# Merge gates of an encoder layer: the sigmoid moved from the merge to the gate projection, as exp, plus one and reciprocal

## The chip, the cores and the metric

The kernel runs on one core of a Trainium2 chip. The core has a matrix engine (TensorE, called PE in the profile; its weight loads have a row of their own, PEld), VectorE (DVE), ScalarE (ACT), GpSimd (POOL) and SyncE (SP), whose queue here issues most DMA transfers. Each engine works through its own instructions in a fixed order and waits on semaphores for the others. PE writes its results to PSUM, from where ACT or DVE must copy or add them out before the same bank is used again.

The metric is the device time of one execution in microseconds. A profile is one such execution, recorded instruction by instruction.

## What is computed

One inference step of one encoder layer for 1024 prompt positions and 64 sample positions (1088 in all), model width 1024. One combined projection of the normalised input gives queries, keys and values, two recurrent inputs, memory queries and, in its last 3072 columns, the logits of three merge gates. Three branches (stick-breaking attention, a gated linear recurrence, cross-attention into a memory) are each projected back to the model width and merged by sigmoid gates, one gate per branch, position and channel:

```python
proj = xn @ lw["w_in"]
...
g = jax.nn.sigmoid(gates.astype(jnp.float32) + lw["b_merge"].astype(jnp.float32)).reshape(b, t, N_BRANCH, D_MODEL)
merged = (g[:, :, 0] * (o_sb @ lw["w_br_sb"]) + g[:, :, 1] * (o_lru @ lw["w_br_lru"])
          + g[:, :, 2] * (o_mem @ lw["w_br_mem"])).astype(x.dtype)
x = x + merged @ lw["w_out"]
```

A SwiGLU feed-forward block follows. All data are float32.

## The kernel before

**Layout and product.** Channels lie on the 128 partitions and positions along the free dimension; a row of 128 channels has T = 1088 positions, in two halves of HT = 544, each of two pieces of HC = 272. Every large product is made with a Strassen-like scheme of seven products instead of eight, on pairs of output rows (256 channels): `sw_weights` (line 149) loads the weights of a pair through SyncE, forms their sums on DVE and splits each into a high and a low part (ACT copies, DVE subtracts: `split`, lines 70 to 73). `sw_steps` (line 182) runs the seven products as fourteen steps, two pieces each, and yields after every step, so that a caller can put other work in between. Line 192 is the matmul. The first three products leave PSUM by an ACT copy into a temporary tile (`keep`, line 202); the other four go through `done`, which calls the caller's `out` for the piece and, after the second piece, the caller's `after` for the half row. All of that stands under `tc.high_priority()`.

Two PSUM pairs are used in turn, so a product needs the pair that was emptied one product earlier. Temporaries are tiles named `swt`; four places serve them in turn and a pair takes two, so two pairs are in flight.

**The projection stage.** `pair_stream` (line 799) runs 24 pairs: eight for the recurrent inputs, four for the memory queries, and last twelve for the merge gates (three branches of four pairs). Its `out` adds the evicted piece to the temporary on DVE (line 809) or copies it out on ACT (line 811). Its `after` stores the half row to a scratch tensor in DRAM on SyncE's queue (line 817): `xl_scr`, `gl_scr`, `q_scr`, and for the gates `g_scr[b][row]`, as raw logits. The weights of the next pair are asked for before the steps of the present one.

The steps of this stream are woven into other work by `bulk.run(n)`: into the eight blocks of the recurrence (lines 860 to 925; each uses ACT's Sigmoid, Tanh, Exp, Sqrt and Gelu) and into the four heads of the memory attention (`mem_attn`, line 982), three steps per token tile. There, `scores` takes a row maximum on DVE (L997), scales it (L999), lets ACT compute the Exp (L1002) and normalises on DVE with a reciprocal (L1003) and a multiply (L1004); `queries` does the query norm (L975 on PE, L977, L244 and L979 on DVE, L245 on POOL). The gate pairs begin in the last block of the recurrence and run through all four heads and beyond. PE's and all other engines' order is fixed when the program is built, by a list scheduler that takes priorities and estimated durations; the hardware doesn't reorder.

**The merge stage.** For each branch and pair of rows, `branch_pair` (line 1124) loads the four half rows of gate logits back (L1128, tiles `sig`, four buffers of the pool tag `stg`) and applies the Sigmoid on ACT with the bias per channel, a column of `prm` from PB = 0 on (L1130). It then runs the projection of the branch; its `out` multiplies each piece by its gate, on POOL after a DVE add (L1136, L1137) or on DVE (L1139), and adds it to `mg` on POOL (L1141). A gate buffer is free for the next pair once its two pieces have been multiplied. After the third branch `form_operands` (line 1096) makes the operands of the output projection from `mg`.

**Table loads.** ACT keeps one set of activation functions at a time; the build puts an ACT_TABLE_LOAD ahead of a function of another set. The profile lists them under the line of the function that needs them.

Of the kernel before, what the change touches and what calls it, by code (L numbers as in the profile page):

```python
# [10 lines left out]
F32 = mybir.dt.float32  # L11
F32R = mybir.dt.float32r
BF16 = mybir.dt.bfloat16
AF = mybir.ActivationFunctionType
ALU = mybir.AluOpType
# [3 lines left out]
P = 128  # L19
D = 1024  # L20
KT = D // P
# [7 lines left out]
MH = 4  # L29
# [7 lines left out]
CQ, CK, CV, CXL, CGL, CQM, CGATE = 0, 1024, 2048, 3072, 4096, 5120, 6144  # L37
# [6 lines left out]
HT = T // 2  # L44
# [5 lines left out]
def kernel(ctx: ExitStack, tc: tile.TileContext, x_prompt, x_sample, mem_prompt, cache_sb_k, cache_sb_v,  # L50
# [6 lines left out]
    V, S, G, TE = nc.vector, nc.scalar, nc.gpsimd, nc.tensor  # L57
    LD, ST = nc.scalar, nc.sync

    cst = ctx.enter_context(tc.tile_pool(name="cst", bufs=1))  # L60
# [121 lines left out]
    def sw_steps(W, X, n, banks, temp, out, mid=None, after=None, fswap=0, hswap=0):  # L182


        def run(op, bank, start):
            a, b = PAIRS[op]
            for c in range(2):
                cs = slice(c * HC, (c + 1) * HC)
                for i in range(n):
                    w, x = W[a], X[b][i]  # L190
                    for j, (wj, xj) in enumerate(((0, 0), (0, 1), (1, 0))):
                        TE.matmul(bank[c][:, :HC], w[:, wj, i], x[:, xj, cs], start=start and i == 0 and j == 0,  # L192
                                  stop=i == n - 1 and j == 2, skip_group_check=True)
                yield c

        def part(j, c=None):
            s = j % 2 * HT + (c or 0) * HC
            return tmp[j // 2][:, s:s + (HT if c is None else HC)]

        def keep(bank, c, j):  # L200
            with tc.high_priority():
                S.copy(part(j, c), bank[c][:, :HC])  # L202

        def done(f, half, bank, c, j):
            with tc.high_priority():
                out(f ^ fswap, half ^ hswap, c, bank[c][:, :HC], part(j, c), j < 3)
                if c and after:
                    after(f, half, part(j))

        bx, bw = banks(), banks()  # L210
        tmp = [temp(), temp()]
        for c in run(0, bx, True):
            keep(bx, c, 0)
            yield
        for c in run(1, bw, True):
            keep(bw, c, 1)
            yield
        for c in run(2, bx, False):
            keep(bx, c, 2)
            yield  # L220
        for c in run(3, bw, False):
            if c == 0 and mid:
                mid()
            done(1, 0, bw, c, 2)
            yield
        for c in run(4, bx, False):
            done(1, 1, bx, c, 1)
            yield
        by = banks()
        for c in run(5, by, True):  # L230
            done(0, 0, by, c, 0)
            yield
        for c in run(6, bx, False):
            done(0, 1, bx, c, 3)
            yield

    def sw_product(*a, **k):
        for _ in sw_steps(*a, **k):
            pass
# [35 lines left out]
    xl_scr = [drm.tile([P, T], F32, name=f"xl{k}") for k in range(KT)]  # L275
    gl_scr = [drm.tile([P, T], F32, name=f"gl{k}") for k in range(KT)]
    q_scr = [drm.tile([P, T], F32, name=f"q{k}") for k in range(KT)]
# [22 lines left out]
    prm = cst.tile([P, 152], F32, name="prm")  # L300
    PB, PCW, PCB, PBA, PBX, PAL, PSC, PSH, PQG = 0, 24, 56, 64, 72, 80, 88, 112, 120
    PNM, PNF, PNE = 128, 136, 144
    tail = cst.tile([P, 8, KT], F32, name="tail")
    clog = cst.tile([P, 8], F32, name="clog")
    nclog = cst.tile([P, 8], F32, name="nclog")


    with ExitStack() as c1:
# [15 lines left out]
        for t in range(NTOK):  # L324
            n = P if t < 8 else DSEQ
# [11 lines left out]
        for g in range(3):  # L337
            for t in range(3 * g, 3 * g + 3):
                xt, n = xts[t]
# [5 lines left out]
            w = min(384, T - c0)  # L345
            for k in range(KT):
                tg = ("z", "tr")[k % 2]
                p = ps.tile([P, 512], F32, tag=tg, name="xp", bufs=3 if tg == "z" else 2)
                for j in range(3):
                    xt, n = xts[3 * g + j]  # L350
                    TE.transpose(p[:, j * P:j * P + n], xt[:n, k * P:(k + 1) * P], ident[:n, :n])
                gk = prm[:, PNM + k:PNM + k + 1]
                for a, b in ((c0, min(c0 + w, HT)), (max(c0, HT), c0 + w)):
                    if a < b:
# [4 lines left out]
                                               op0=ALU.mult, op1=ALU.subtract)  # L359
# [308 lines left out]
        pt = ps.tile([P, 512], F32, tag="tr", name="prt1", bufs=2)  # L668
        TE.transpose(pt[:, :122], pr1[:122, :], ident[:122, :122])
        V.tensor_copy(prm[:, :122], pt[:, :122])  # L670

        def x_sums():

            for i in range(KT // 2):
                def quarter(k, half):
                    q = sb.tile([P, HT], F32, tag="xq", name=f"xq{k}{half}", bufs=3)
                    u = xq(k, half)
                    V.tensor_add(q, f32(u[:, 0]), f32(u[:, 1]))
                    return q

                k0, k1 = 2 * i, 2 * i + 1
                t3 = quarter(k1, 1)
                yield
                t1 = quarter(k0, 1)
                yield
                V.tensor_sub(t3, t3, t1)
                ST.dma_start(s_scr[i]["T3"], t3)
                yield
                t2 = quarter(k0, 0)
                yield  # L690
                V.tensor_sub(t1, t1, t2)
                ST.dma_start(s_scr[i]["T1"], t1)
                yield
                V.tensor_add(t2, t2, t3)
                ST.dma_start(s_scr[i]["T2"], t2)
                yield
                t4 = quarter(k1, 0)
                yield
                V.tensor_sub(t4, t4, t2)
                ST.dma_start(s_scr[i]["T4"], t4)  # L700
                yield
# [27 lines left out]
    NI = KT // 2  # L729
# [26 lines left out]
    def half(name):  # L756
        return wpl.tile([P, HT], F32, tag="stg", name=name, bufs=4)
# [3 lines left out]
    def operand_at(oi, i, name):  # L761
        return at(UNITS[oi * NI + i], name).rearrange("p (x n) -> p x n", x=2)
# [15 lines left out]
    X = {o: A.get(o, []) for _, o in PAIRS}  # L778
    for oi, (_, o) in enumerate(PAIRS):
        if o[0] == "T":  # L780
            for i in range(NI):
                t = operand_at(oi, i, f"x{o}{i}")
# [6 lines left out]
    def temp():  # L789
        return at(cycle("t", TEMPS), "swt", F32)  # L790
# [8 lines left out]
    def pair_stream(pairs, last):  # L799

        def weights(i):
            if i == len(pairs):
                return last()
            cols, _, nm = pairs[i]
            return sw_weights([w_in[0, :, c:c + P] for c in cols], nm, w_slot, w_stage)

        def out(f, hf, c, p, t, add):
            if add:
                V.tensor_add(t, p, t)  # L809
            else:  # L810
                S.copy(t, p)

        w = weights(0)
        for i, (_, dst, _) in enumerate(pairs):
            wn = weights(i + 1)
            yield from sw_steps(w, X, NI, banks4, temp, out,
                                after=lambda f, hf, t: ST.dma_start(dst[f][:, hf * HT:(hf + 1) * HT], t))
            w = wn
        stream["w"] = w

    stream = {}
    pairs = [((CXL + n * P, CGL + n * P), (xl_scr[n], gl_scr[n]), f"wl{n}_") for n in range(KT)]
    pairs += [((CQM + 2 * m * P, CQM + (2 * m + 1) * P), (q_scr[2 * m], q_scr[2 * m + 1]), f"wq{m}_") for m in range(MH)]
    pairs += [((CGATE + b * D + 2 * j * P, CGATE + b * D + (2 * j + 1) * P), (g_scr[b][2 * j], g_scr[b][2 * j + 1]),
               f"wg{b}{j}_") for b in range(3) for j in range(NI)]

    with ExitStack() as c2:
        mk = c2.enter_context(tc.tile_pool(name="mk", bufs=2))
# [27 lines left out]
    with ExitStack() as c2:  # L856
# [3 lines left out]
        for n in range(KT):  # L860
# [14 lines left out]
            for s, m in LSEG:  # L875
                a = s + (3 if s else 0)
                V.tensor_scalar(xc[:, s:s + m], xl[:, a:a + m], prm[:, PCW + n:PCW + n + 1], col(PCB),
                                op0=ALU.mult, op1=ALU.add)
                for i in range(1, 4):
                    V.scalar_tensor_tensor(xc[:, s:s + m], xl[:, a + i:a + i + m],  # L880
                                           prm[:, PCW + 8 * i + n:PCW + 8 * i + n + 1], xc[:, s:s + m],
                                           op0=ALU.mult, op1=ALU.add)
# [191 lines left out]
    if True:  # L1074
# [45 lines left out]
        def piece(hf, c):  # L1120
            return slice(hf * HT + c * HC, hf * HT + (c + 1) * HC)


        def branch_pair(b, j, W, X):
            sig = {}
            for f, hf in ((0, 1), (0, 0), (1, 1), (1, 0)):
                st = sig[f, hf] = half(f"sig{f}{hf}")
                ST.dma_start(st, g_scr[b][2 * j + f][:, hf * HT:(hf + 1) * HT])  # L1128
                k = PB + 8 * b + 2 * j + f
                S.activation(st, st, AF.Sigmoid, bias=prm[:, k:k + 1])  # L1130

            def out(f, hf, c, p, t, add):
                d = mg[2 * j + f][:, piece(hf, c)]
                g = sig[f, hf][:, c * HC:(c + 1) * HC]
                if add:
                    V.tensor_add(t, p, t)  # L1136
                    G.tensor_mul(t if b else d, t, g)  # L1137
                else:
                    V.tensor_mul(t if b else d, p, g)  # L1139
                if b:  # L1140
                    G.tensor_add(d, d, t)  # L1141

            sw_product(W, X, NI, banks4, temp, out, fswap=1, hswap=1)
# [3 lines left out]
        X = load_branch(0)  # L1147
        for b in range(3):
# [9 lines left out]
            if b < 2:  # L1158
                X = load_branch(b + 1)
        tt = [at(p, "tt", F32).rearrange("p (x n) -> p x n", x=2) for p in (RAW, SPARE[3])]  # L1160
        X = form_operands(mg, [tt[i // 2][:, i % 2] for i in range(NI)], "xm")
# [166 lines left out]
        for q, (gi, j) in enumerate(steps):  # L1328
            if j == 0:
                X = load_operands([h_scr[i] for i in groups[gi]], f"h{gi}")  # L1330
# [40 lines left out]
```

## Time and profile before

| | |
|---|---|
| Median of three runs | 2401.46 us (2393.33 to 2403.85) |
| The profiled execution's own time | 2398.64 us |
| Its span, first to last instruction | 2396.9 us |
| Mean granted TensorE clock | 0.984 of full speed |
| First and last start of a gate store (L817) | 935.7 and 1269.2 us |
| First and last start of a gate reload (L1128) | 1197.9 and 1516.6 us |
| First and last start of a gate Sigmoid (L1130) | 1202.6 and 1522.8 us |
| Table loads of line 1130 | 4, from 1201.3 to 1287.3 us |

How the views are read: a row of instruction groups gives the line in the kernel, engine, operation, the tiles (result and operands) with their shapes and the count; then busy microseconds and the mean nanoseconds of one; then how long the engine stood idle just before them and what ended that. A row of waits names who waited for whom, the total, how often, and the longest. A row of windows gives a stretch of the span, its length, and the busy time and number of instructions of PE, PEld, DVE, ACT and POOL, then the granted clock, the DMA share and GB/s. The view of one line gives counts with minimum, median and maximum in nanoseconds and the first and last start.

### The profile page before, as it was taken

What the parts mean: (1) busy time and instruction counts of PE and PEld (TensorE: products, weight loads), DVE (VectorE), ACT (ScalarE), POOL (GpSimd) and SP (SyncE); (2) the same over time, 40 slices, a digit from 0 to 9 for tenths busy, and PEclk for the clock granted to TensorE, in tenths of its full rate; (3) what the DMA queues carried; (4) which work ended last, traced back from release to release, by engine and by line L of the source; (5) the groups of instructions that cost most, each with busy time, mean ns of one, the idle gap of its engine ahead of it and who ended that gap; (6) DMA issues with size and microseconds to landing.
All of it is one profiled execution on the core that took longest, in us unless ns stands there. A gap on an engine that the chain in (4) does not pass through costs nothing.

```text
span 2396.9 us, 44723 instructions
## 1 busy us (share of the span) xinstructions
PE 2267.3 (95%) x17429; PEld 2200.5 (92%) x17429; DVE 1635.7 (68%) x2877; ACT 1221.6 (51%) x2481; POOL 750.6 (31%) x715
## 2 busy tenths in 40 slices
PE   7999999997999999999999998898999999999998
PEld 6888888887999999999999998797999999999998
DVE  6765665666667768766557857678666666687884
ACT  5455555565465566555556644456333333353553
POOL 2223232335222331111111356725334344340110
PEclk9999999998999999999999999999999999999999
DMA  5212121233544453444456655233323233263543
GB/s 176 88 53 76 44 68 53 76 89 117 185 138 149 131 170 122 143 133 134 138 174 199 209 168 168 72 111 110 96 86 110 87 100 105 89 220 117 166 139 88
DMA packets 328650, 293.26 MB, mean 122 GB/s; under 512 B 19427, under 2 KB 259254, under 8 KB 328438
## 3 DMA queue, kind: packets, MB, share of 16 engines
q1 hardware_dynamic: 286360, 269.35, 34.9%
q10 hardware_dynamic: 42078, 21.05, 3.0%
q8 instruction: 137, 2.24, 0.4%
q14 instruction: 75, 0.61, 0.1%
HBM read 194.34 MB, written 95.99 MB: 121 GB/s over the span
## 4 chain that ended last, share of the span: by engine, by line
PE 52%; DVE 9%; POOL 5%; DMA 4%; issue 4%; ACT 2%; SPq 0%; ACTq 0%; POOLq 0%; DVEq 0%
PE sw L192 46%; POOL swt L1137 1%; DMA sig<-g 1%; POOL mg L1141 1%; DVE xc L880 1%; PE ssq L975 1%; PE avm L99 0%; DVE x2T L73 0%; DVE h0T L73 0%; DVE x1T L73 0%; DVE xgT L73 0%; PE gt L99 0%; DMA o1B<-gl 0%; PE sc L101 0%; PE sc L100 0%
## 5 line engine op out<-in xcount | busy, mean ns | idle before, releaser
L202 ACT COPY swt<-sw 128x272 f32<-128x272 f32 x444 | 168.8, 385 | 221.0 <-PE sw L192 219.8
L1261 POOL TENSOR_TENSOR u<-u,R 128x272 f32<-128x272 f32 x66 | 66.4, 1006 | 172.4 <-DVE u L1260 165.2
L192 PE MATMUL sw<-xT,wg_S 128*128 128x272 f32 x864 | 119.4, 290 | 0.0
L192 PEld LDWEIGHTS sw<-xT,wg_S 128*128 128x128 f32 x864 | 111.5, 188 | 0.0
L452 DVE SCALAR_TENSOR_TENSOR e<-z,e 128x384 f32<-128x384 f32 (+4 forms) x96 | 50.9, 552 | 81.1 <-ACT e L450 80.7
L453 DVE TENSOR_TENSOR_SCAN e<-ones,e 128x128 f32<-128x128 f32 (+3 forms) x64 | 95.0, 1492 | 0.6
L809 DVE TENSOR_TENSOR swt<-sw,swt 128x272 f32<-128x272 f32 x144 | 61.7, 434 | 46.0 <-PE sw L192 45.3
L1300 POOL TENSOR_TENSOR y<-y,swt 128x272 f32<-128x272 f32 x18 | 18.3, 1018 | 213.5 <-DVE swt L1299 213.5
L192 PE MATMUL sw<-B,wg_A 128*128 128x272 f32 x576 | 81.0, 290 | 0.0
L192 PE MATMUL sw<-xT,wl_S 128*128 128x272 f32 x576 | 78.1, 292 | 0.6 <-ACT xT L72 0.5
L1270 ACT ACTIVATE sil<-sil 128x272 f32<-128x272 f32 x88 | 37.5, 429 | 79.2 <-POOL sil L1261 71.4
L192 PEld LDWEIGHTS sw<-xT,wl_S 128*128 128x128 f32 x576 | 75.5, 192 | 1.1 <-ACT xT L72 0.7
L192 PEld LDWEIGHTS sw<-B,wg_A 128*128 128x128 f32 x576 | 75.0, 188 | 0.0
L1277 DVE TENSOR_TENSOR u<-u,sil 128x272 f32<-128x272 f32 x88 | 39.4, 448 | 49.9 <-POOL u L1261 49.2
L73 DVE TENSOR_TENSOR al<-at,ah 128x128 fp32r<-128x128 f32 (+2 forms) x96 | 51.6, 549 | 30.1 <-ACT ah L72 30.1
L1261 POOL TENSOR_TENSOR sil<-sil,R 128x272 f32<-128x272 f32 x66 | 50.0, 779 | 61.6 <-DVE sil L1260 58.6
L457 ACT ACTIVATE e<-e 128x128 f32<-128x128 f32 (+3 forms) x64 | 43.8, 685 | 48.5 <-DVE e L456 36.6
L1137 POOL TENSOR_TENSOR swt<-swt,sig 128x272 f32<-128x272 f32 x48 | 47.9, 999 | 65.7 <-DVE swt L1136 65.7
L245 POOL TENSOR_TENSOR ri<-ri,mhalf 128x2 f32<-128x2 f32 (+1 forms) x20 | 13.4, 670 | 162.3 <-DVE ri L244 155.2
L72 ACT CAST ah<-at 128x128 fp32r<-128x128 f32 (+2 forms) x96 | 44.3, 479 | 36.7 <-PE at L505 36.6
L1141 POOL TENSOR_TENSOR mg<-mg,swt 128x272 f32<-128x272 f32 x64 | 61.4, 968 | 4.8 <-DVE swt L1139 1.0
L1130 ACT ACTIVATE sig<-sig,prm 128x544 f32<-128x544 f32 x48 | 35.6, 751 | 52.5 <-DMA sig<-g 47.0
(1588 smaller groups left out, 7991.5 us busy)
## 6 DMA issues: line engine op xcount, KB each, us to landing
g<-swt SPq DMA_DIRECT2D x48, 272.0 KB
sig<-g SPq DMA_DIRECT2D x48, 272.0 KB
wg_r<-in_w_in_dram SPq DMA_DIRECT2D x48, 256.0 KB
hT<-u SPq DMA_DIRECT2D x44, 272.0 KB
hB<-u SPq DMA_DIRECT2D x33, 272.0 KB
out_dram<-kvs SPq DMA_DIRECT2D x32, 256.0 KB
wl_r<-in_w_in_dram SPq DMA_DIRECT2D x32, 256.0 KB
sT<-xq SPq DMA_DIRECT2D x16, 272.0 KB
```

What stands on the lines that cost most here:

```text
L72: (h_eng or S.copy)(h, src)
L73: (l_eng or V).tensor_sub(l, src, f32(h))
L192: TE.matmul(bank[c][:, :HC], w[:, wj, i], x[:, xj, cs], start=start and i == 0 and j == 0, stop=i == n - 1 and j == 2, skip_group_check=True)
L202: S.copy(part(j, c), bank[c][:, :HC])
L452: V.scalar_tensor_tensor(ev, z, 0.0, ev, op0=ALU.max, op1=ALU.add)
L453: V.tensor_tensor_scan(e[:, ::-1], ones1[:n].to_broadcast([n, L]), e[:, ::-1], 0.0, op0=ALU.mult, op1=ALU.add)
L457: S.activation(e, e, AF.Exp)
L809: V.tensor_add(t, p, t)
L1137: G.tensor_mul(t if b else d, t, g)
L1141: G.tensor_add(d, d, t)
L1261: G.tensor_mul(d, d, r)
L1277: ffn_out(u, lambda f, hf, c, d: V.tensor_mul(d, d, sil[f][:, piece(hf, c)])), hswap=1)
```

## The change

The gates are finished where they are projected. The list of pairs gets a fourth entry, the column of the bias for gate pairs and None for all others. The function called after each finished half row (`put`) now, for gate pairs, computes in place exp(-(t + bias)) on ACT with the negated bias as operand, adds one and takes the reciprocal on DVE, and then stores the half row as before; this is 1 / (1 + exp(-x)), the sigmoid. The negated biases are a new small tile `nbm` (128 x 24), filled once by DVE. In `branch_pair` the loaded half rows are used as they are; the Sigmoid is gone. Count, size and queue of the transfers stay.

```diff
+    nbm = cst.tile([P, 24], F32, name="nbm")
...
         V.tensor_copy(prm[:, :122], pt[:, :122])
+        V.tensor_scalar(nbm, prm[:, PB:PB + 24], -1.0, None, op0=ALU.mult)
...
+        def put(f, hf, t):
+            if bias is not None:
+
+                S.activation(t, t, AF.Exp, scale=-1.0, bias=nbm[:, bias + f:bias + f + 1])
+                V.tensor_scalar(t, t, 1.0, None, op0=ALU.add)
+                V.reciprocal(t, t)
+            ST.dma_start(dst[f][:, hf * HT:(hf + 1) * HT], t)
+
         w = weights(0)
-        for i, (_, dst, _) in enumerate(pairs):
+        for i, (_, dst, _, bias) in enumerate(pairs):
             wn = weights(i + 1)
-            yield from sw_steps(w, X, NI, banks4, temp, out,
-                                after=lambda f, hf, t: ST.dma_start(dst[f][:, hf * HT:(hf + 1) * HT], t))
+            yield from sw_steps(w, X, NI, banks4, temp, out, after=put)
...
     pairs += [((CGATE + b * D + 2 * j * P, CGATE + b * D + (2 * j + 1) * P), (g_scr[b][2 * j], g_scr[b][2 * j + 1]),
-               f"wg{b}{j}_") for b in range(3) for j in range(NI)]
+               f"wg{b}{j}_", 8 * b + 2 * j) for b in range(3) for j in range(NI)]
...
                 ST.dma_start(st, g_scr[b][2 * j + f][:, hf * HT:(hf + 1) * HT])
-                k = PB + 8 * b + 2 * j + f
-                S.activation(st, st, AF.Sigmoid, bias=prm[:, k:k + 1])
```

More of the change, by code (lines that the diff above doesn't have):

```diff
@@ L803, in weights @@
                 return last()
-            cols, _, nm = pairs[i]
+            cols, _, nm, _ = pairs[i]
             return sw_weights([w_in[0, :, c:c + P] for c in cols], nm, w_slot, w_stage)
@@ L821 @@
     stream = {}
-    pairs = [((CXL + n * P, CGL + n * P), (xl_scr[n], gl_scr[n]), f"wl{n}_") for n in range(KT)]
-    pairs += [((CQM + 2 * m * P, CQM + (2 * m + 1) * P), (q_scr[2 * m], q_scr[2 * m + 1]), f"wq{m}_") for m in range(MH)]
+    pairs = [((CXL + n * P, CGL + n * P), (xl_scr[n], gl_scr[n]), f"wl{n}_", None) for n in range(KT)]
+    pairs += [((CQM + 2 * m * P, CQM + (2 * m + 1) * P), (q_scr[2 * m], q_scr[2 * m + 1]), f"wq{m}_", None) for m in range(MH)]
     pairs += [((CGATE + b * D + 2 * j * P, CGATE + b * D + (2 * j + 1) * P), (g_scr[b][2 * j], g_scr[b][2 * j + 1]),
-               f"wg{b}{j}_") for b in range(3) for j in range(NI)]
+               f"wg{b}{j}_", 8 * b + 2 * j) for b in range(3) for j in range(NI)]
     with ExitStack() as c2:
```

## The prediction

> **What bounds the kernel now.** I read the page's engine totals first, then the windows around the gate projection and the merge, because the change moves work from the second to the first.
>
> ```profile
> span 2396.9 us, 44723 instructions
> PE 2267.3 (95%) x17429; PEld 2200.5 (92%) x17429; DVE 1635.7 (68%) x2877; ACT 1221.6 (51%) x2481; POOL 750.6 (31%) x715
> ```
> TensorE (PE) is busy 95% of the span. Work on another engine costs nothing while it stays in PE's shadow, and costs its excess once it doesn't.
>
> ```profile
> core 0: us, PE busy (x) PEld busy (x) DVE busy (x) ACT busy (x) POOL busy (x), PEclk, DMA share, GB/s
> 935.00:985.00 50.00, 47.24 (x371) 46.70 (x370) 37.82 (x56) 29.36 (x52) 13.51 (x10) 1.00 0.49 162
> 985.00:1237.00 252.00, 251.90 (x2001) 244.87 (x1999) 152.43 (x406) 136.68 (x326) 31.52 (x32) 1.00 0.40 128
> 1237.00:1300.00 63.00, 61.66 (x490) 61.22 (x490) 46.69 (x77) 38.04 (x78) 10.53 (x9) 1.00 0.76 250
> 1300.00:1525.00 225.00, 214.41 (x1677) 212.87 (x1677) 157.68 (x248) 118.45 (x228) 111.66 (x117) 0.98 0.53 167
> 1525.00:1565.00 40.00, 24.65 (x144) 23.16 (x143) 31.56 (x37) 18.09 (x34) 31.94 (x25) 0.83 0.14 40
> ```
> The three upper rows cover the gate projection: the last LRU block, the four memory heads, and the tail with the start of branch 0. In the memory stage PE never rests (251.9 of 252 us) and VectorE (DVE) has 99.6 us of idle time. The two lower rows are the merge, where PE loses 10.6 and 15.4 us. What stands in front of that loss:
>
> ```profile
> PE sw L192 <- ACT swt L202: 9.7, 4, 3.5
> PE sw L192 <- DVE swt L1136: 7.4, 4, 3.8
> PE sw L192 <- ACT xmB L72: 4.3, 1, 4.3
> ...
> ACT sig L1130 <- DMA sig<-g: 43.3, 22, 4.2
> ```
> These are the waits from 1300 to 1565 us (total, times, longest). The Sigmoid on ScalarE (ACT) waits 43.3 us for reloaded gates, and the PSUM copies of line 202 stand behind it on ACT; PE waits for those copies. That part of the merge the change can improve.
>
> **What it removes.**
>
> ```profile
> L1130 ACT ACTIVATE sig<-sig,prm 128x544 f32<-128x544 f32 x48 | 35.6, 751 | 52.5 <-DMA sig<-g 47.0 <-POOL mg L1141 5.4
> L1002 ACT ACT_TABLE_LOAD x4 | 5.1, 1283 | 0.1
> L1130 ACT ACT_TABLE_LOAD x4 | 5.1, 1283 | 2.8 <-DMA sig<-g 2.8
> ```
> From the merge go 48 Sigmoids of 0.751 us (35.6 us of ACT), their waits, and the table loads by which Sigmoid and the softmax's Exp displace each other: four of line 1130 and three of the four of line 1002, 7 x 1.283 = 9.0 us of ACT. PE can get back at most the two eviction waits above, 9.7 + 7.4 = 17.1 us; at least nothing, because the reloaded gate is still awaited, now by POOL's multiply (L1137) or DVE's (L1139), and POOL's chain of multiply and add is late next. I take 10 us, a little over half: ACT's blocked queue goes, the load's landing time and the buffers' turnover stay.
>
> **What it adds.** Each of 48 half-rows (128x544) gets an Exp on ACT, then an add and a reciprocal on DVE, before its store. The Exp has the Sigmoid's form and takes 0.751 us. For DVE the nearest rows are:
>
> ```profile
> L1003 DVE RECIPROCAL sm<-sm 128x1 f32<-128x1 f32 x32 | 5.2, 161 | 12.0 <-ACT pe L1002 11.8
> L1003 DVE RECIPROCAL sm<-sm 64x1 f32<-64x1 f32 x4 | 0.6, 148 | 0.0
> L839 DVE RECIPROCAL sp<-sp 128x8 f32<-128x8 f32 x1 | 0.2, 196 | 0.0
> ...
> L977 DVE COPY ssq_s<-ssq 128x2 f32<-128x2 f32 x16 | 2.5, 156 | 19.3 <-PE ssq L975 19.3
> L1004 DVE TENSOR_SCALAR pe<-pe,sm 128x256 f32<-128x256 f32 x32 | 11.2, 352 | 1.0
> L343 DVE TENSOR_SCALAR x<-x,rx 128x1024 f32<-128x1024 f32 x8 | 6.0, 752 | 4.0 <-POOL rx L245 4.0
> L845 DVE TENSOR_SCALAR sp<-sp 128x8 f32<-128x8 f32 x8 | 1.3, 166 | 0.1
> ```
> The add: (752 - 352) / 768 = 0.52 ns per element, so 352 + 288 x 0.52 = 0.50 us. The reciprocal is the open price, for the trace has none longer than 8 elements. An ordinary 128x8 operation takes 166 ns, the reciprocal 196, while at one element it costs no more than a two-element copy: it is not a fixed surcharge but a price per element. With a fixed part of 152 ns (between 148 and 156) it is (196 - 152) / 8 = 5.5 ns, and 152 + 544 x 5.5 = **3.1 us**, which I take. Low end: from 128x1 to 128x8, with the 128x1 median of 164 ns, (196 - 164) / 7 = 4.6 ns, 2.65 us. High end: that median less the copy's 156, 8 ns for one element, 4.5 us. Were there no price per element beyond the add's, it would be 0.5 us; the 196 ns speak against that.
>
> ```profile
> L1003 DVE RECIPROCAL sm<-sm x36: 147/164/166, 987.2 to 1229.6; 128x1 f32<-128x1 f32 x32, 64x1 f32<-64x1 f32 x4
> ```
> (This row, of line 1003 alone, has the median.) The Trainium skill bears on this price: "VectorE: DVE Perf Modes", section "Walkthrough: the 8-slice pipeline in each mode", says that the reciprocal is an iterative divide with a repeat count of 8. At the page's 0.96 GHz that would be 8.3 ns an element, by estimate 4.7 us for 544, and the sum below would come out near the dear rival's. The 128x8 row agrees in kind (a price per element) but gives 5.5 ns, and no run here shows a long one.
>
> So a half-row costs DVE 0.5 + 3.1 = 3.6 us, and 48 cost 173 us. Where they fall I count from the present stores, in the view of line 817 by window:
>
> ```profile
> L817 SPq DMA_DIRECT2D g<-swt x9: 320/338/454, 935.7 to 982.8; - x9
> ...
> L817 SPq DMA_DIRECT2D g<-swt x32: 319/338/710, 987.3 to 1236.9; - x32
> ...
> L817 SPq DMA_DIRECT2D g<-swt x8: 319/320/458, 1236.9 to 1269.2; - x8
> ```
> The one at 1236.9 is in two windows, so 9, 32 and 7. DVE's idle time can take them only as far as it isn't the answer to DVE's own earlier work:
>
> ```profile
> DVE wg_A L73 <- ACT wg_A L72: 7.1, 2, 5.3
> DVE th L913 <- POOL a L909: 2.2, 1, 2.2
> ...
> DVE ssq_s L977 <- PE ssq L975: 26.5, 16, 2.9
> DVE swt L809 <- PE sw L192: 18.4, 24, 1.3
> DVE ri L979 <- POOL ri L245: 12.5, 16, 0.9
> DVE mx L997 <- PE sc L101: 11.9, 18, 1.5
> DVE sm L1003 <- ACT pe L1002: 11.8, 22, 1.1
> ...
> DVE wb01A L73 <- ACT wb01A L72: 4.0, 2, 3.1
> ```
> Waits for PE vanish when DVE is the late one. Waits for POOL and ACT to answer DVE (12.5 + 11.8 = 24.3 us in the memory stage) stay. For the outer windows I keep half of such waits, an estimate: 6 us each.
>
> - Last LRU block: 37.8 + 9 x 3.6 + 6 = 76 us of DVE in a window of 50: +26.
> - Memory stage: 152.4 + 32 x 3.6 + 24.3 = 292 us in 252: +40.
> - Tail: 46.7 + 7 x 3.6 + 6 = 78 us in 63: +15.
>
> Together +81 us, all of which PE feels: its next product needs the PSUM pair that the add of line 809 empties, and that add stands in DVE's queue behind a reciprocal. With 10 us back from the merge it is +71: 2398.64 (the profiled execution's own time) + 71 = **2470 us**. That execution is 0.1% under the median of 2401.46, less than the rounding here, so I leave it.
>
> **Edits costed at nothing.** The negated bias (nbm) is one small DVE operation of about 0.17 us, once, under PE work. The moved Exps add 32 x 0.751 = 24 us to ACT's 136.7 of 252: covered; without that cover the copies of line 202 would be late by up to 0.75 us each. In the last LRU block nine Exps come among Sigmoid, Gelu and Sqrt; their stores stand in two groups, so two to four table loads, 2.6 to 5.1 us, and ACT goes from 29.4 to about 41 of 50. The new wait of the add for its Exp holds DVE's in-order queue, with the next evictions behind it; by the row of line 1003 such a wait is about half a microsecond (11.8 / 22), and I let the scheduler put other work into it. The store now waits on SyncE for 0.75 + 0.5 + 3.1 = 4.4 us longer. Behind it stand the next pair's weights (L157) and the query and key loads (L965, L939):
>
> ```profile
> SPq L817 <- DVE swt L809: 40.5, 30, 7.6
> SPq L157 <- DVE swt L809: 39.0, 6, 11.9
> SPq L939 <- DVE ql L73: 25.3, 3, 9.3
> ```
> Weights are asked for one pair ahead, and PE waits for no load in the memory stage; that covers it. The four swt tiles are two pairs' worth, so a store that is 4 us late frees its tile in time.
>
> **The rivals.**
> Dear reciprocal: at 4.5 us a half-row costs 5.0. The windows become 37.8 + 45 + 6 = 89 (+39), 152.4 + 160 + 24.3 = 337 (+85) and 46.7 + 35 + 6 = 88 (+25): +149, and with nothing from the merge 2547 us. For it: the one-element rows allow 8 ns. Against: 128x8 gives less.
>
> Packed queue: the reciprocal at 2.65 us, no DVE wait left, the merge giving its 17: 37.8 + 28 = 66 (+16), 152.4 + 101 = 253 (+1), 46.7 + 22 = 69 (+6), so +23 - 17 = +6, 2405 us. For it: most of DVE's idle time is waiting for PE. Against: the order is fixed beforehand, and every softmax step goes DVE, ACT, DVE.
>
> Faster: the cover holds. In the memory stage DVE can take (252 - 152.4 - 24.3) / 32 = 2.35 us per half-row; below a reciprocal of 1.85 us, 3.2 ns an element, nothing stalls there, and the merge's 10 to 17 us remain: about 2385 us. For it: the merge's waits are real, and ACT sheds table loads. Against: the 196 ns.
>
> The change without its purpose: the loads' wait only moves to POOL, and the merge gives nothing: 2480 us. It is inside the forecast.
>
> **How the numbers follow.** Forecast (2425 to 2510) 0.58, dear reciprocal (2510 to 2560) 0.22, packed queue (2395 to 2425) 0.10, faster 0.10. A measurement of this kernel tells about 0.5% from no change, 12 us. Of the packed case most falls inside 2389 to 2413: same 0.08; faster 0.09; slower 0.83. The range runs from the packed case's 2405 to 2540, just short of the dear end, leaving out the faster case, the low part of the packed one and the last of the dear one.
>
> **What would show it.** Right: a RECIPROCAL row of 128x544, x48, near 3.1 us; DVE's total near 1809 us; PE waits for swt of line 809 between 935 and about 1380 us, where there were none in the memory stage; in the merge no ACT work on sig, and fewer waits for L202. Wrong: a reciprocal under 1.85 us (then faster), or over 4 us (then dearer); PE still full from 985 on; or a merge that is longer than its present 265 us because the gates arrive late.

## The result, and the profile after

The changed kernel takes 2465.97 us (median of four runs, 2460.71 to 2472.59), the kernel before 2402.65 in the same comparison. The ratio is 1.0277, with a 95% interval of 1.0251 to 1.0302: slower by 63 us. The forecast was 2470. In the changed kernel the lines lie a little further down: 809 is 811 there, 817 is 821, 1002 is 1011 and 1136 is 1143.

The first part of the page of the changed kernel:

```profile
span 2465.3 us, 44784 instructions
PE 2286.7 (93%) x17429; PEld 2216.7 (90%) x17429; DVE 1804.4 (73%) x2974; ACT 1218.3 (49%) x2476; POOL 762.8 (31%) x715
```

DVE went from 1635.7 to 1804.4 us. ACT is level: its Sigmoids left and as many Exps came. The three operations of a finished half row, from the groups by form, and the small tile, from the view of its line:

```profile
L820 DVE RECIPROCAL swt<-swt 128x544 f32<-128x544 f32 x48 | 168.7, 3534 | 0.0
L819 DVE TENSOR_SCALAR swt<-swt 128x544 f32<-128x544 f32 x48 | 21.3, 446 | 1.2 <-ACT swt L818 1.2
...
L818 ACT ACTIVATE swt<-swt,nbm 128x544 f32<-128x544 f32 x48 | 35.8, 751 | 24.9 <-DVE swt L811 24.7
```
```profile
L672 DVE TENSOR_SCALAR nbm<-prm x1: 1721/1721/1721, 79.7 to 79.7; 128x24 f32<-128x24 f32 x1
```

The reciprocal takes 3.53 us for 544 elements; against the 161 ns of one element that is (3534 - 161) / 543 = 6.2 ns per element.

To compare the stages I cut both traces at the same work: from 935 us to the first product of branch 0 that takes the operand x0T and the weights wb00A (start 1276.2 before, 1357.6 after), and from there to the product of the output projection that takes xmT and wo0A (1568.0 and 1638.1). The windows before, then after:

```profile
935.00:1276.20 341.20, 338.34 (x2683) 330.77 (x2682) 218.78 (x510) 190.15 (x428) 49.46 (x45) 1.00 0.47 152
1276.20:1568.00 291.80, 264.51 (x2019) 261.05 (x2018) 210.41 (x317) 152.31 (x291) 149.69 (x148) 0.96 0.47 149
```
```profile
935.00:1357.60 422.60, 360.67 (x2697) 349.59 (x2696) 379.66 (x603) 217.83 (x475) 54.06 (x45) 0.91 0.39 128
1357.60:1638.10 280.50, 263.17 (x2019) 260.07 (x2018) 219.10 (x323) 120.74 (x239) 154.70 (x148) 0.96 0.48 147
```

The gate stage (first row of each) grew by 422.6 - 341.2 = 81.4 us, the merge (second row) shrank by 291.8 - 280.5 = 11.3. In the gate stage DVE is now busy 90% of the time. It got 160.9 us more work; its idle time fell from 122.4 to 42.9 us and took 79.5 of that; the rest is the 81.4 us. PE, which had lost 2.9 us there, now loses 61.9, and its granted clock is 0.91, so that the same products keep it busy 22 us longer. What it waits for in the gate stage of the changed kernel, each row with total, times and longest:

```profile
PE ptp L1020 <- DVE ri L244: 17.2, 2, 8.6
PE sw L192 <- DVE x0B L73: 12.5, 1, 12.5
PE sw L192 <- ACT wg_S L72: 9.7, 1, 9.7
PE sc L99 <- ACT pe L1011: 7.1, 3, 4.2
PE ptp L1020 <- DVE pe L1013: 6.5, 3, 6.0
...
PE sw L192 <- DVE swt L811: 0.5, 1, 0.5
```

The first row puts two waits of 8.6 us to a query norm of a few elements (L244). It stood in DVE's queue behind reciprocals. PE did nothing from 1184.1 to 1192.7 us, and this is DVE's order there:

```profile
1185.22 6.96 DVE L820 RECIPROCAL swt<-swt 128x544 f32<-128x544 f32 x2
1192.09 0.11 DVE L1012 RECIPROCAL sm<-sm 128x1 f32<-128x1 f32 x1
1192.12 0.14 DVE L986 COPY ssq_s<-ssq 128x2 f32<-128x2 f32 x1
1192.24 0.35 DVE L1013 TENSOR_SCALAR pe<-pe,sm 128x256 f32<-128x256 f32 x1
1192.51 0.16 DVE L244 TENSOR_SCALAR ri<-ssq_s 128x2 f32<-128x2 f32 x1
```

The last row of PE's waits matters too: the add that empties a PSUM pair (line 811) made PE wait 0.5 us in the whole stage. PE waited for other work that stood behind reciprocals in DVE's queue: small steps of the attention, sums of weights, and the splits of x0B. What DVE itself still waited for there, its longest waits:

```profile
DVE ssq_s L986 <- PE ssq L984: 14.7, 13, 2.8
DVE ri L988 <- POOL ri L245: 9.6, 18, 0.8
DVE swt L811 <- PE sw L192: 5.8, 7, 1.4
DVE mx L1006 <- PE sc L101: 2.5, 4, 1.0
```

In the merge PE's waits for ACT's copies of line 202 fell to 1.3 us, from 11.0 in the same stretch before (9.7 of them behind 1300 us):

```profile
PE sw L192 <- DVE swt L1143: 6.9, 4, 3.8
...
PE sw L192 <- ACT swt L202: 1.3, 1, 1.3
```

### The profile page after: what moved, and what is told of

The parts are those of the page before. It is cut to its first block, busy times and chain, and to the rows that moved or that the text cites. A ratio compares the mean times of both kernels' runs of the same rounds, so it can differ in the third digit from the quotient of the medians.

```text
span 2465.3 us, 44784 instructions
## 1 busy us (share of the span) xinstructions
PE 2286.7 (93%) x17429; PEld 2216.7 (90%) x17429; DVE 1804.4 (73%) x2974; ACT 1218.3 (49%) x2476; POOL 762.8 (31%) x715
## 4 chain that ended last, share of the span: by engine, by line
PE 43%; DVE 10%; issue 2%; POOL 2%; DMA 1%; ACT 1%; SPq 0%; POOLq 0%; ACTq 0%; DVEq 0%
PE sw L192 39%; DVE swt L820 3%; PE ssq L984 1%; DVE h0T L73 0%; DVE x2T L73 0%; DVE x1T L73 0%; PE sc L99 0%; PE avm L99 0%; DVE xgT L73 0%; PE ptp L1020 0%; PE sc L100 0%; PE sc L101 0%; PE avm L100 0%; DVE h2T L73 0%; PE avm L101 0%
## 5 line engine op out<-in xcount | busy, mean ns | idle before, releaser
L820 DVE RECIPROCAL swt<-swt 128x544 f32<-128x544 f32 x48 | 168.7, 3534 | 0.0
L192 PE MATMUL sw<-xT,wg_S 128*128 128x272 f32 x864 | 125.3, 296 | 9.7 <-ACT wg_S L72 9.7
L1268 POOL TENSOR_TENSOR u<-u,R 128x272 f32<-128x272 f32 x66 | 66.1, 1002 | 171.7 <-DVE u L1267 164.5
L453 DVE SCALAR_TENSOR_TENSOR e<-z,e 128x384 f32<-128x384 f32 (+4 forms) x96 | 50.9, 552 | 79.8 <-ACT e L451 79.5
L811 DVE TENSOR_TENSOR swt<-sw,swt 128x272 f32<-128x272 f32 x144 | 60.2, 431 | 34.4 <-PE sw L192 32.7
```

Source lines behind the costliest of these rows:

```text
L453: V.scalar_tensor_tensor(ev, z, 0.0, ev, op0=ALU.max, op1=ALU.add)
L820: V.reciprocal(t, t)
L1268: G.tensor_mul(d, d, r)
```

## The experiments

Theory A: the loss is the sum of DVE's work in the gate stage. DVE's idle time takes new work until it is used up; from there each microsecond of DVE is one of the kernel. The rivals: the Exp on ACT and the later stores cost the time (B); single evictions blocked behind a long reciprocal (C); the merge's gain is only apparent (D); the scheduler's order (E); ACT's table loads (F); no kink, each reciprocal costs its share (G). Medians stand beside the ratio to the kernel before in the same comparison, with its 95% interval. The median of the kernel before was 2402.65 us in the first comparison and 2394.5 to 2397.3 in the later ones, so the ratios compare better than the times.

### No reciprocal

```diff
-                V.reciprocal(t, t)
```

> The changed kernel without the 48 reciprocals (the gates are then 1 + exp(-x), so the output differs); Exp, add, store and the merge without Sigmoid stay. Theory A (DVE's time is the bound: 48 x 3.53 us of reciprocal exceed what DVE has idle in the gate stage): in the memory stage DVE needs 152.4 + 32 x 0.45 + 24.3 = 191 of 252 us, nothing stalls, the merge's gain stays: 2380 to 2396 us. Rival B (the Exp on ACT, its wait in DVE's queue and the later stores cost the time): still above 2440 us.

2391.75 us, ratio 0.9987 (0.9973 to 1.0001). Exp, add and late stores are all there, and the loss is gone. So the loss is the reciprocals', and B falls as its cause. The rest isn't free, though: the merge alone gives back more (0.9956, below), so some 0.3% or 7 us are lost elsewhere. The gate stage of this kernel, to the same product of branch 0, is 9.4 us longer than before:

```profile
935.00:1285.60 350.60, 342.83 (x2701) 335.12 (x2699) 240.26 (x562) 212.42 (x470) 49.96 (x45) 0.99 0.46 148
```

### Two reciprocals

```diff
                 V.reciprocal(t, t)
+                V.reciprocal(t, t)
```

> The changed kernel with a second reciprocal behind the first (the gates are then 1 + exp(-x), so the output differs). Theory A: DVE has been full already, so each further microsecond of it is a microsecond of the kernel: 48 x 3.53 = 170 us more, 2466 + 170 = 2636 us, 2610 to 2660. Rival C (the loss is the blocking of single evictions behind a reciprocal, and part of each still hides): about half of it, 2550 us.

2629.89 us, ratio 1.0971 (1.0945 to 1.0996): by the medians 164 us more than with one, by the ratios 166. The second set's own row, and the gate stage of this kernel to the same product of branch 0:

```profile
L821 DVE RECIPROCAL swt<-swt 128x544 f32<-128x544 f32 x48 | 166.2, 3505 | 0.0
```
```profile
935.00:1522.00 587.00, 376.71 (x2680) 364.09 (x2679) 544.92 (x646) 213.65 (x472) 53.69 (x44) 0.80 0.28 92
```

166 us of DVE cost 164 to 166 us of the kernel, and DVE's idle time is 42.1 us, as with one reciprocal (42.9). DVE had been full: what is left idle doesn't shrink under more work. That is theory A without a remainder.

### Half the reciprocals

```diff
-                V.reciprocal(t, t)
+                if f:
+                    V.reciprocal(t, t)
```

> The changed kernel with the reciprocal on only two of a pair's four half rows, 24 in place of 48 (the other gates are 1 + exp(-x), so the output differs). It looks for the kink. Theory A (DVE's idle time takes work until it is used up): from 935 us to the first product of branch 0 with new operands DVE worked 379 us in the changed kernel and kept 43 idle; less 24 x 3.45 us that is 296 + 43 = 339, less than the 351 us that this stretch takes without any reciprocal: 2388 to 2402 us. Rival G (no kink: each reciprocal costs its share because it delays an eviction): half of the 74 us between none and 48, 2422 to 2435 us.

2400.62 us, ratio 1.0011 (0.9997 to 1.0026). The first 24 reciprocals (85 us of DVE) cost 1.0011 - 0.9987, about 6 us; the next 24 cost 1.0277 - 1.0011, about 64. The kink is there, and G falls. The row of those 24, and the gate stage of this kernel:

```profile
L821 DVE RECIPROCAL swt<-swt 128x544 f32<-128x544 f32 x24 | 85.1, 3546 | 0.1
```
```profile
935.00:1283.40 348.40, 340.81 (x2662) 330.00 (x2660) 296.21 (x567) 207.14 (x464) 49.19 (x45) 1.00 0.45 147
```

DVE has 52.2 us idle here, close to the 42 at which it is full, and PE's clock is still 1.00.

### The same work in another order

Outside the scheduler's high priority 42 of the 48 reciprocals stand singly in DVE's order, where the changed kernel has most of them two and three in a row; the last four still stand together, before branch 0. (The stores of the other pairs keep the high priority; that part of the edit is left out here.)

```diff
                 out(f ^ fswap, half ^ hswap, c, bank[c][:, :HC], part(j, c), j < 3)
-                if c and after:
-                    after(f, half, part(j))
+            if c and after:
+                after(f, half, part(j))
...
```

> The changed kernel with the Exp, add, reciprocal and store of a gate issued outside the scheduler's high priority. The same instructions run; in the built order of DVE the reciprocals of a pair, which stand two and three in a row in the changed kernel, now stand singly among other work. Theory A (only the sum of DVE's work counts): within 12 us of the changed kernel, 2450 to 2480 us. Theory E (part of the loss is order: blocks of about 16 us of reciprocals, behind which PE was seen to wait 8.6 us twice, 6.0 and 9.7 us): those about 33 us and the clock lost after them come back, 2425 to 2445 us.

2463.87 us, ratio 1.0281 (1.0251 to 1.0311): no change. PE waits in other places (the longest is now 20.7 us before branch 0, the two of 8.6 are gone), and DVE's work and idle time in the stage are the same:

```profile
PE sw L192 <- DVE x0B L73: 20.7, 1, 20.7
```
```profile
935.00:1357.80 422.80, 362.08 (x2692) 349.13 (x2691) 381.26 (x602) 215.93 (x474) 52.80 (x45) 0.92 0.40 128
```

E falls for this order. The waits of 8.6 us were where the shortage showed, not its cause. It also answers a doubt about the run with half the reciprocals, in which all 24 stand singly: standing singly isn't what made them cheap. The next run cuts each reciprocal in four, so that other work could go in between every microsecond:

```diff
-                V.reciprocal(t, t)
+                for c in range(4):
+                    V.reciprocal(t[:, c * P:(c + 1) * P + 32 * (c == 3)], t[:, c * P:(c + 1) * P + 32 * (c == 3)])
```

> The changed kernel with each reciprocal cut into four, three of 128 elements and one of 160. The work is the same but for three more fixed parts of 0.06 to 0.15 us each, 9 to 22 us of DVE in all; another instruction can go in between every microsecond. Theory A (sum of DVE's work): 2470 to 2488 us. Rival C (blocks of 3.5 us in an in-order queue): 2420 to 2450 us. The row of 128 elements also settles the price per element.

2474.27 us, ratio 1.0310 (1.0285 to 1.0334), as theory A has it. Against C this run says little, for the built order mostly leaves the pieces together; here eight stand in a row:

```profile
1114.26 7.21 DVE L821 RECIPROCAL swt<-swt 128x128 f32<-128x128 f32 x8
```

C falls by other figures: twice the reciprocals cost their full time and not half, and in the changed kernel PE waits 0.5 us in all for the adds that empty its PSUM pairs. The rows give the price again, (3534 - 914) / 416 = 6.3 ns per element:

```profile
L821 DVE RECIPROCAL swt<-swt 128x128 f32<-128x128 f32 x144 | 124.9, 914 | 0.1
L821 DVE RECIPROCAL swt<-swt 128x160 f32<-128x160 f32 x48 | 50.8, 1103 | 0.0
```

### The merge alone

The kernel before, without its Sigmoid:

```diff
                 ST.dma_start(st, g_scr[b][2 * j + f][:, hf * HT:(hf + 1) * HT])
-                k = PB + 8 * b + 2 * j + f
-                S.activation(st, st, AF.Sigmoid, bias=prm[:, k:k + 1])
```

> The kernel before with the Sigmoid left out of the merge and nothing put in its place (the gates are raw logits, so the output differs). It measures what the merge alone gives back. The prediction took 10 us and the trace of after suggests 12 (the first product of branch 1 starts 82 us later, that of the output projection 70): 2403 - 10 to - 14, 2388 to 2394 us. Rival D (the merge is bound by POOL's chain and the landing of the loads, and the 12 us in the trace are slack that the late start of branch 0 filled): 2399 to 2405 us.

2385.46 us, ratio 0.9956 (0.9943 to 0.9970): 0.44%, 9 to 11 us, close to the 11.3 of the trace after. The time itself lies below the 2388 to 2394 expected, which were counted from 2403; the kernel before had 2394.5 in this comparison. The gain is real and D falls. The gates are still loaded back here, and no engine is seen to wait for those loads, here or in the changed kernel.

### Versions that finish the gates early without a reciprocal

Tanh gives the same function with one pass on DVE:

```diff
-                S.activation(t, t, AF.Exp, scale=-1.0, bias=nbm[:, bias + f:bias + f + 1])
-                V.tensor_scalar(t, t, 1.0, None, op0=ALU.add)
-                V.reciprocal(t, t)
+                S.activation(t, t, AF.Tanh, scale=0.5, bias=nbm[:, bias + f:bias + f + 1])
+                V.tensor_scalar(t, t, 0.5, 0.5, op0=ALU.mult, op1=ALU.add)
```

Here `nbm` holds half the bias. The other versions change one thing each: the pass on POOL, no high priority, or the Sigmoid itself on ACT (there `nbm` holds the bias); the last has the Sigmoid without the high priority.

> The same function at the same place with the reciprocal avoided: Tanh of half the logit plus half the bias on ACT, then times 0.5 plus 0.5 on DVE in one pass. Theory A: DVE adds 48 x 0.45 = 21 us, covered as in the kernel without reciprocals; Tanh costs ACT what Exp does, and in the built order it needs two table loads of its own, none in the memory stage: 2380 to 2396 us, faster than both kernels. Rival B (the early finishing itself costs, by ACT's part or the late stores): above 2440 us.

> The Tanh version with its last pass (times 0.5 plus 0.5) on POOL in place of DVE, so that DVE does no more than in the kernel before. The Tanh version came out at 0.9987 of the kernel before, though the merge alone gives 0.9956. If the 7 us between are DVE's 21 us in the gate stage: 2384 to 2388 us. If they come from the Tanh's place on ACT or from the order at the first memory head (PE waited 4.7 and 2.4 us there): 2390 to 2395 us, as with DVE.

> The Tanh version with Tanh, pass and store outside the scheduler's high priority. If the 7 us that the Tanh version loses against the merge's own gain come from gate work that overtakes the first memory head's in the fixed order: 2384 to 2388 us. If they are the price of 21 us more DVE and 36 us of ACT in a stage where PE has no idle time: 2390 to 2395 us.

> The same place with the Sigmoid itself: one ACT function per half row, nothing on DVE. In the built order ACT loads tables 24 times for it and 21 times for the softmax's Exp, 45 x 1.283 = 58 us of ACT, of which the kernel before had 8. Theory A (DVE alone is the bound, ACT has 115 us idle in the memory stage): 2384 to 2396 us. Rival F (a load stands in ACT's queue ahead of the softmax's Exp and of the PSUM copies, and PE, which has no idle time there, waits): 2400 to 2440 us.

> The early Sigmoid on ACT with gate work outside the scheduler's high priority. The early Sigmoid with priority came out at 0.9974 of the kernel before and the Tanh version without priority at the same, the merge alone at 0.9956. If what is missing is gate work overtaking the softmax in the fixed order: 0.995 to 0.997; if it is ACT's table loads, which stay at 45: 0.997 to 0.999.

| Version | Median, us | Ratio to before, interval |
|---|---|---|
| Tanh, pass on DVE | 2392.46 | 0.9987 (0.9974 to 1.0000) |
| Tanh, pass on POOL | 2392.13 | 0.9993 (0.9977 to 1.0008) |
| Tanh, no high priority | 2390.36 | 0.9974 (0.9960 to 0.9988) |
| Sigmoid early | 2389.54 | 0.9974 (0.9961 to 0.9986) |
| Sigmoid early, no high priority | 2387.67 | 0.9955 (0.9939 to 0.9970) |

The last beats both kernels, the one before by 0.45%, and keeps all of the merge's gain. F had put the early Sigmoid at 2400 us or more, and falls. The table loads and the window to 1237 us in the last version:

```profile
L818 ACT ACT_TABLE_LOAD x24 | 30.8, 1283 | 0.4
L1012 ACT ACT_TABLE_LOAD x21 | 26.9, 1283 | 0.4
```
```profile
935.00:1237.00 302.00, 297.05 (x2342) 289.71 (x2341) 190.45 (x456) 229.84 (x448) 45.80 (x41) 0.99 0.41 132
```

The loads take 57.7 us, 43 of the 45 in this window. ACT is busy 229.8 of 302 us, and PE loses 5.0, against 2.9 before. Why the Tanh versions stay 0.2 to 0.4% behind the merge alone isn't settled. The version on POOL came out like that on DVE, which speaks against DVE's 21 us. In the profiled executions PE waits 3.4 to 4.7 us at the first memory head (4.7 for a query norm in the first Tanh version), but intervals of neighbouring versions overlap, and no run tests that wait alone.

## Why the prediction was right

**The bound of the stage.** Step: DVE has idle time that takes gate work up to a point; above it PE feels all. Right, and the runs with none, half, all and twice the reciprocals (ratios 0.9987, 1.0011, 1.0277, 1.0971) show the kink between half and all. The forecast put it at 2.35 us of DVE per half row; half the reciprocals are an average of 1.77 + 0.45 = 2.22 us and cost about 6 us, all of them 3.98. (The same sum puts the reciprocal's price there at (1853 - 152) / 544 = 3.1 ns an element, not 3.2.)

**How PE feels it.** Wrong: the forecast had PE wait for the PSUM pair that the add of line 809 empties, and named such waits as the sign. Of the 61.9 us that PE lost in the gate stage the trace puts 0.5 us to that add (L811). The waits are for the attention's steps on DVE (17.2 us at the query norm, 6.5 at L1013), for the Exp between them on ACT (7.1), for x0B (12.5) and for weights (9.7, whose sum on DVE stood behind reciprocals). A full DVE delays all that it feeds, and PE stood at what came due next in its own order.

**The reciprocal's price.** Taken: 3.1 us with ends of 2.65 and 4.5, from two rows of 1 and 8 elements. Measured: 3.53. A price per element read from a difference of 44 ns (196 less 152) came out 12% below the measured reciprocal. The Trainium skill's repeat count of 8 ("VectorE: DVE Perf Modes", section "Walkthrough: the 8-slice pipeline in each mode") gave an estimate of 4.7 us; the trace agrees that it is a price per element, but at 6.2 ns and not 8.3, and the measurement decides.

**The sum.** It came out as +81 against a measured +81.4 by errors that cancelled, which is luck. The work was put too high: a half row costs 0.446 + 3.534 = 3.98 us and not 3.6, about 191 us for 48 and not 173, but DVE's busy time in the stage rose by only 160.9. Two things make up the 30 us between. DVE's instructions overlap (last section): the sum of their durations exceeds the busy time by 41.9 us in this stage, and by 21.7 before, and I had added durations as if they stood alone. And DVE's other work there sums to 230.5 us where it had been 240.5, in part because seven splits of x0T and x0B now fall behind the cut.

The idle time that takes the work was put too high by as much: 128 us in the three windows less 36 kept are 92, and it took 79.5. The 42.9 us that stayed are near the 36, but not by the reason given. I had kept DVE's waits for POOL and ACT and let those for PE vanish. In the trace after, 24.9 us of the 42.9 are waits for PE, 14.7 of them for the sums of the query norm, and 16.1 for POOL and ACT. The 81 us are also those of one profiled pair: by the medians the kernel lost 63 and not 71.

**The places.** Wrong: I gave +26 to the last LRU block, +40 to the memory stage and +15 to the tail. The first memory score came 49.9 us later (980.2, then 1030.1), the last one 66.7 (1221.9, then 1288.6), the first product of x0T and wb00A 81.4. So the shares were about 50, 17 and 15. The failed step is counting the half rows by the stores of the old trace. Before the first score 8 half rows had been stored then, and 13 in the changed kernel, and 13 x 3.98 = 52 us. The fixed order had put more gate work ahead of the attention.

**The merge.** Taken 10 us, measured 11.3 in the trace and 0.44% in the run of its own. The cause was the one named, ACT's queue standing behind the reloads: of the two waits counted, the one for the copies of line 202 nearly went, and the one for line 1136 (1143 after) stayed, 7.4 and 6.9 us. The late wait for the gates at POOL or DVE, which was to eat part of the gain, doesn't appear.

**Edits at nothing.** Exps, adds and stores: nearly, for the run without reciprocals keeps some 7 us less than the merge alone gives, and no run shows which of them costs that. The bias tile took 1.72 us and not 0.17, under PE's work. The new wait of the add for its Exp is 1.2 us in all 48.

## What to carry to other kernels

Count an edit against the idle time of the engine it lands on, in the stage where it lands, less what of it will stay idle even when the engine is full. Here that was about 42 us, with one reciprocal and with two, and more of it was waiting for PE than the forecast allowed. Up to there the work costs little (6 us for 85 us of reciprocals), beyond it it costs one for one, and the one change of order that was tried won nothing. Before replacing a function that one engine does in a single pass by a chain on another, price the longest link per element: here the division cost 4.7 times the whole Sigmoid (3.534 against 0.751 us), while the Sigmoid itself fitted at the same place, table loads included. To test such a reading, take the suspected work away, halve it and double it: the kink tells a full engine from a delayed one.

## What the runs showed of the hardware

DVE's instructions overlap when they stand close. In the changed kernel passes of 0.68 us start 0.60 us apart:

```profile
1006.00 0.68 DVE L174 TENSOR_TENSOR wg_s<-wg_r,wg_r 128x512 f32<-128x512 f32 x1
1006.60 0.68 DVE L172 TENSOR_TENSOR wg_s<-wg_r,wg_s 128x512 f32<-128x512 f32 x1
1007.20 0.69 DVE L73 TENSOR_TENSOR wg_S<-wg_s,wg_S 128x512 fp32r<-128x512 f32 x1
```

So a sum of durations overstates a full queue by some 12% for passes of this size; reciprocals of 3.53 us in a row start 3.46 us apart, 2%.

A switch of ACT's table costs little more than the load. In the version with the early Sigmoid and no high priority the copy ends at 1064.25, and the Exp starts 1.31 us later:

```profile
1063.86 0.39 ACT L202 COPY swt<-sw 128x272 f32<-128x272 f32 x1
1064.26 1.28 ACT L1012 ACT_TABLE_LOAD   x1
1065.56 0.56 ACT L1012 ACTIVATE pe<-sc,mx,ri 128x256 f32<-128x256 f32 x1
```

The Trainium skill, "ScalarE: Activation LUTs", section "Table sets: the hidden batching unit", counts about 2.7 us for each load and advises to batch by set. The trace shows 1.31 us for a switch, and the measurement decides. In this kernel 45 such switches left the ratio where the merge alone puts it (0.9955 and 0.9956).

PE's clock fell after a wait. In the changed kernel PE stood still for 9.7 us until 1006.8 us, and the next 8 us ran at a granted clock of 0.75:

```profile
996.90:1006.80 9.90, 0.20 (x3) 0.01 (x1) 9.90 (x7) 1.07 (x3) 0.00 (x0) 0.69 0.19 71
1006.80:1015.00 8.20, 8.20 (x50) 8.00 (x51) 8.20 (x12) 3.70 (x8) 1.84 (x1) 0.75 0.49 145
1015.00:1024.00 9.00, 9.00 (x74) 9.00 (x74) 9.00 (x11) 2.91 (x5) 8.36 (x6) 1.00 0.55 189
```

Over the gate stage, at a mean clock of 0.91, PE's work took 22 us longer. With two reciprocals the clock was lower still, 0.80, and DVE stood idle no longer than with one (42.1 and 42.9 us). So I take it that the lower clock cost nothing on top; no run changes the clock alone.
